# One decoder layer on one core: the output projection with its tokens stationary, the residual stream in rows, and the second norm's scale found beside its transposes

## The chip, the core and the metric

The kernel runs on one core of a Trainium2 chip. The metric is device microseconds of one execution. The kernel is written with a manual schedule: every engine works through its instructions in the order in which the Python code issues them. The engines are TensorE (PE in the profile, its weight loads PEld), VectorE (DVE), ScalarE (ACT), GpSimd (POOL) and SyncE (SP), which issues nearly all DMA transfers.

## The reference

One layer for 256 tokens (S) of width 2048 (D), all in fp32. `c` is one conditioning vector, and `mod` its six modulation vectors of width D.

```python
mod = (silu(c) @ ada_w + ada_b)                # sh1, sc1, g1, sh2, sc2, g2
h = rms_norm(x, norm1_g) * (1 + sc1) + sh1
u, lru_gate, q, k, v, mix_gates = split(h @ w_in + b_in)
y_lru  = rg_lru(causal_conv(u)) * gelu(lru_gate)
y_attn = sliding_window_attention(q, k, v, sinks)
gate_lru, gate_attn = split(sigmoid(mix_gates))
merged = gate_lru * (y_lru @ w_lru_out) + gate_attn * (y_attn @ w_attn_out)
x = x + g1 * (merged @ w_o)                    # called x1 below
h2 = rms_norm(x, norm2_g) * (1 + sc2) + sh2
gate, up = split(h2 @ w_ffn_in)
x = x + g2 * ((silu(gate) * up) @ w_ffn_out)
out = rms_norm(x, final_g)
```

The change concerns the line of `w_o` and the one that makes `h2`.

## The kernel before

**Products in three.** Each fp32 operand is split into a rounded "hi" and a remainder "lo", and a product is made as hi·hi + hi·lo + lo·hi (`mm3`, lines 319 to 321). The split of the activations is done once. The weights are split as they come.

**Items.** A weight matrix is cut into slabs of 512 output columns (`add_slab`), and a slab into items of 128 partitions x 1024 elements (512 KB), which hold two blocks of 128 contraction rows. Each item is loaded by SyncE into one of five buffers (`do_load`, tile `raw`, line 265), cast by ACT into `hi` (`do_hi`, line 274), subtracted by DVE into `lo` (`do_lo`, line 286), and multiplied. `step(i)` issues the load of item i+5, the cast and the subtraction of items a few ahead, and then the products of item i. So loads run five items ahead of the products. Eight items make a slab of 2048 contraction rows; a slab sums in two PSUM banks.

**Which operand stands.** `add_slab` has two forms. By default the weights are loaded into the array (128x128) and the 256 tokens move through: the result has output columns on the partitions and tokens along them. With `in_rows=True` the tokens are stationary, in two halves of 128, and 512 weight columns move: the result has tokens on the partitions. Tiles `wi`, `wl`, `wa` and `wo` are the banks of `w_in`, `w_lru`, `w_att` and `w_o`; `fg` and `fu` are the two halves of `w_ffn_in`. Up to the change w_o uses the first form, and w_att the second.

**Side work.** The modulation vectors are found meanwhile: 158 tiles `aw` of 512 KB are loaded from `ada_t` (line 377, three buffers) and each is multiplied with the spread `silu(c)` and summed in one DVE pass (line 406) into a column of `modc`, where `modc[:, m, kt]` is vector m (2 is g1, 3 is sh2, 4 is (1+sc2)·norm2_g) for output columns 128·kt onward. A planner keeps an estimated clock for each engine (`charge`, `load_time`) and puts such passes between items where its estimate has room; generators in `posts` (what is to be done after a slab: `o_post` for w_o) yield costs and are advanced once an item. What the planner decides is fixed when the program is built.

**Stages around the change.** The products of w_att (`wa`) begin at 656.6 us, those of w_o (`wo`) at 754.1 us, and those of w_ffn_in (`fg`) at 853.8 us. In w_o, `o_post(0)` issues four loads of x, transposed (`load_x`, line 123), behind the loads that `step` has issued by then; after each of the first three slabs DVE forms x1 = x + g1·(merged @ w_o) in place (line 958: g1 is a number for each partition), ACT squares it, and DVE adds the squares up over blocks into `fs`.

**The gap ahead of h2.** After the last slab `second_norm` has DVE finish x1, ACT square it, TensorE sum the squares over the partitions by products with a matrix of ones (tile `r`, lines 954 and 963; the sums come out spread over all partitions), ACT take the root (line 965), and DVE the reciprocal (line 966, 128x256). Then DVE scales (`scaled`, line 979) and ACT shifts and rounds (`high`, line 983) two blocks at a time, and DVE makes the remainders (`low`). h2 must have its first blocks before `fg` begins; the later blocks are made item by item in `rest`. Meanwhile TensorE transposes x1 back into rows (`rows_of`, line 934, 32 transposes), and ACT copies them out for writes to DRAM (`x1d`), from where the last stage reads x1.

Of the kernel before, what the change touches and what calls it, by code (L numbers as in the profile page):

```python
# [47 lines left out]

N_PIECES, N_F, K_FIRST = 3, 4, 3
# [16 lines left out]
def hybrid_layer(  # L66
    ctx: ExitStack, tc, vecs, x_t, c_row, ada_k, ada_t, ada_g, w_in, bv_row, bm_row, bg_row, lru_w, w_lru, w_att, w_o,
# [37 lines left out]
    def rows(t):  # L105
        return slice(t * P, (t + 1) * P)
# [32 lines left out]
    warm = mtile("warm")  # L139
    for _ in range(N_WARM):  # L140
        nc.tensor.matmul(warm[:, 0:P], lhsT=ones, rhs=ones, start=True, stop=True)
    free(m=1)
# [742 lines left out]
    for i in range(4):  # L885
        add_slab(w_in[SL_GA + i], f"wga{i}", hact, 0, NK, gate_post(SL_GA + i, i, ga), True, load_gate_bias(SL_GA + i), 4)
    for s in range(4):
        add_slab(w_att[s], f"wa{s}", aact, 0, NK, att_post(s), True)
# [3 lines left out]
    x1T, second = [], {}  # L892

    def o_post(s):
        def post(banks):
            if s == 0:
                x1T.extend(load_x("x1T"))
                second["fs"] = b4("fs2")
            if s == 3:
                second_norm(banks)  # L900
                return
            if s == 2:
                early_root()
            yield 0, 0
# [12 lines left out]
        return post  # L917
# [9 lines left out]
    pts = {}  # L927

    def rows_of(i, of_w=False):

        s, t = divmod(i, 2)
        pt = wtile(f"ptx{i}").rearrange("p j n -> p (j n)") if of_w else mtile(f"ptx{i}")
        for j in range(4):
            nc.tensor.transpose(pt[:, j * P:(j + 1) * P], x1T[s][:, j, rows(t)], ident)
        pts[i] = (pt, 0 if of_w else 1)

    def rows_out(i):
        s, t = divmod(i, 2)
        pt, m = pts.pop(i)
        xr = b4(f"xr{i}", F32, (512,))  # L940
        nc.scalar.copy(xr, pt)
        nc.sync.dma_start(x1d[rows(t), s * 512:(s + 1) * 512], xr)
        free(b4=1, m=m)
# [3 lines left out]
    def second_norm(banks):  # L947
        sides[:] = [ada_ffn]
        fs = second["fs"]
        both = h2["both"] = hp.tile([P, NK, 2, S], F32R, tag="h", name="h2_both")  # L950
        hh, hl = both[:, :, 0, :], both[:, :, 1, :]
        ps = mtile("r2_ps")[:, 0:S]
        for s in range(3):
            nc.tensor.matmul(ps, lhsT=ones, rhs=fs[:, s, :], start=s == 0, stop=False, skip_group_check=True)
        sq = b4("sq3")
        for f in range(4):
            xf = x1T[3][:, f, :]
            nc.vector.scalar_tensor_tensor(
                xf, banks[f // 2][:, f % 2, :], modc[:, 2, 12 + f:13 + f], xf, op0=ALU.mult, op1=ALU.add
            )  # L960
            nc.scalar.activation(sq[:, f, :], xf, AF.Square)
        for f in range(4):
            nc.tensor.matmul(ps, lhsT=ones, rhs=sq[:, f, :], start=False, stop=f == 3, skip_group_check=True)
        r2 = b4("r2")[:, 0, :]
        nc.scalar.activation(r2, ps, AF.Sqrt, bias=eps_t, scale=1.0 / D)
        nc.vector.reciprocal(r2, r2)
        free(m=1)

        for i in range(6):
            rows_of(i, i in (3, 4))  # L970
        for i in range(4):
            rows_out(i)
            if i < 2:
                rows_of(6 + i)

        def scaled(p):
            for kt in (2 * p, 2 * p + 1):
                xk = x1T[kt // 4][:, kt % 4, :]
                nc.vector.scalar_tensor_tensor(xk, xk, modc[:, 4, kt:kt + 1], r2, op0=ALU.mult, op1=ALU.mult)

        def high(p):
            for kt in (2 * p, 2 * p + 1):
                nc.scalar.activation(
                    hh[:, kt, :], x1T[kt // 4][:, kt % 4, :], AF.Identity, bias=modc[:, 3, kt:kt + 1]
                )

        def low(p):
            for kt in (2 * p, 2 * p + 1):
                nc.vector.scalar_tensor_tensor(
                    hl[:, kt, :], x1T[kt // 4][:, kt % 4, :], modc[:, 3, kt:kt + 1], f32(hh[:, kt, :]),  # L990
                    op0=ALU.add, op1=ALU.subtract,
                )

        def rest():
            for p in range(NK // 2):
                if 0 < p < 4:
                    rows_out(4 + p)
# [369 lines left out]
```

## Time and profile before

| | us |
|---|---|
| median of 3 runs | 1594.91 |
| lowest, highest | 1591.74, 1596.39 |
| the profiled execution | 1598.15 |
| its span | 1596.3 |
| its mean granted TensorE clock | 0.995 of full |

The profile is of one execution, and the times in its rows are microseconds from the start of its span. A row of a timeline gives the start, the time it took, the engine, the line, the operation with its output and inputs, a count if several like instructions stand in a row, and in brackets the idle time before it and what ended it. A product's row gives its whole passage through the array; the next one starts before it ends, so the spacing of starts is the time that a product costs. A line number is that of the program before. Bytes moved: 399.36 MB, 250 GB/s as a mean over the span.

### The profile page before, as it was taken

What the parts mean: (1) busy time and instruction counts of PE and PEld (TensorE: products, weight loads), DVE (VectorE), ACT (ScalarE), POOL (GpSimd) and SP (SyncE); (2) the same over time, 40 slices, a digit from 0 to 9 for tenths busy, and PEclk for the clock granted to TensorE, in tenths of its full rate; (3) what the DMA queues carried; (4) which work ended last, traced back from release to release, by engine and by line L of the source; (5) the groups of instructions that cost most, each with busy time, mean ns of one, the idle gap of its engine ahead of it and who ended that gap; (6) DMA issues with size and microseconds to landing.
All of it is one profiled execution on the core that took longest, in us unless ns stands there. A gap on an engine that the chain in (4) does not pass through costs nothing.

```text
span 1596.3 us, 22536 instructions
## 1 busy us (share of the span) xinstructions
PE 1571.4 (98%) x8522; PEld 1358.2 (85%) x8522; DVE 1124.5 (70%) x1427; ACT 770.2 (48%) x973; POOL 4.8 (0%) x9
## 2 busy tenths in 40 slices
PE   8999999999999999999999999999999999999997
PEld 5999999998888887878998887888888888888886
DVE  6789988989988888788757877445545544444465
ACT  4754444485965455333446444444444444333343
POOL 0000000000000000000000000000000000000000
PEclk9999999999999999999999999999999999999999
DMA  8998998767588778989967899666666666656553
GB/s 306 332 341 311 333 338 280 269 217 240 194 277 283 247 274 274 312 294 315 338 184 222 306 334 321 185 187 188 194 186 188 194 186 229 234 195 195 190 196 119
DMA packets 113586, 399.36 MB, mean 250 GB/s; under 512 B 12611, under 2 KB 13763, under 8 KB 113093
## 3 DMA queue, kind: packets, MB, share of 16 engines
q1 hardware_dynamic: 113190, 397.41, 75.2%
q8 instruction: 66, 1.08, 0.3%
q10 hardware_dynamic: 288, 0.52, 0.1%
q14 instruction: 42, 0.34, 0.1%
HBM read 393.69 MB, written 4.19 MB: 249 GB/s over the span
## 4 chain that ended last, share of the span: by engine, by line
PE 86%; DMA 8%; DVE 4%; issue 1%; ACT 0%; SPq 0%; DVEq 0%; ACTq 0%
PE pf L1089 11%; PE wi L321 6%; PE wi L319 6%; PE wi L320 6%; PE fg L319 4%; PE fg L320 4%; PE fg L321 4%; PE fu L320 4%; PE fu L321 4%; PE fu L319 4%; PE pl L1089 3%; DMA aw<-in_ada_t_dram 3%; DMA aw<-in_ada_g_dram 3%; PE wo L320 2%; PE wo L319 2%; PE wo L321 2%
## 5 line engine op out<-in xcount | busy, mean ns | idle before, releaser
L274 ACT CAST hi<-raw 128x1024 fp32r<-128x1024 f32 (+1 forms) x552 | 565.3, 1027 | 764.4 <-PE pf L1089 109.8
L286 DVE TENSOR_TENSOR lo<-raw,hi 128x1024 fp32r<-128x1024 f32 (+1 forms) x552 | 655.1, 1192 | 349.3 <-PE pf L1089 95.7
L321 PE MATMUL wi<-h_both,lo 128*128 128x256 f32 x784 | 222.1, 283 | 1.1 <-DVE lo L286 1.1
L319 PE MATMUL wi<-h_both,hi 128*128 128x256 f32 x784 | 222.6, 284 | 0.0
L320 PE MATMUL wi<-h_both,hi 128*128 128x256 f32 x784 | 221.8, 283 | 0.0
L321 PEld LDWEIGHTS wi<-h_both,lo 128*128 128x128 f32 x784 | 150.5, 192 | 1.5 <-DVE lo L286 1.5
L319 PEld LDWEIGHTS wi<-h_both,hi 128*128 128x128 f32 x784 | 150.5, 192 | 0.2
L320 PEld LDWEIGHTS wi<-h_both,hi 128*128 128x128 f32 x784 | 150.5, 192 | 0.2
L319 PE MATMUL fg<-hi,h_both 128*128 128x512 f32 x352 | 139.1, 395 | 0.0
L320 PE MATMUL fu<-lo,h_both 128*128 128x512 f32 x352 | 137.2, 390 | 1.0 <-DVE lo L286 1.0
L320 PE MATMUL fg<-lo,h_both 128*128 128x512 f32 x352 | 137.3, 390 | 0.0
L321 PE MATMUL fg<-hi,h_both 128*128 128x512 f32 x352 | 137.2, 390 | 0.0
L321 PE MATMUL fu<-hi,h_both 128*128 128x512 f32 x352 | 137.0, 389 | 0.0
L319 PE MATMUL fu<-hi,h_both 128*128 128x512 f32 x352 | 136.9, 389 | 0.0
L406 DVE CUSTOM_DVE_ANT_0 aw<-aw,crow,modc 128x1024 f32<-128x1024 f32 x79 | 101.1, 1281 | 19.3 <-DMA aw<-in_ada_t_dram 19.0
L406 DVE CUSTOM_DVE_ANT_0 aw<-aw,crow,vec 128x1024 f32<-128x1024 f32 x79 | 100.9, 1280 | 19.4 <-DMA aw<-in_ada_t_dram 19.1
L1089 PE MATMUL pf<-hi,fh 128*128 128x512 f32 x264 | 88.5, 389 | 0.0
L1089 PE MATMUL pf<-hi,fl 128*128 128x512 f32 x264 | 88.4, 389 | 0.0
L1089 PE MATMUL pf<-lo,fh 128*128 128x512 f32 x264 | 88.4, 389 | 0.0
L320 PEld LDWEIGHTS fu<-lo,h_both 128*128 128x128 f32 x352 | 66.1, 188 | 15.5 <-DVE lo L286 1.8
L320 PEld LDWEIGHTS fg<-lo,h_both 128*128 128x128 f32 x352 | 66.1, 188 | 14.6 <-issue 0.7
L319 PEld LDWEIGHTS fg<-hi,h_both 128*128 128x128 f32 x352 | 66.1, 188 | 14.2 <-issue 0.7
(233 smaller groups left out, 2615.1 us busy)
## 6 DMA issues: line engine op xcount, KB each, us to landing
raw<-in_w_f_dram SPq DMA_DIRECT2D x176, 512.0 KB, 3.6
raw<-in_w_in_dram SPq DMA_DIRECT2D x160, 512.0 KB, 6.8
aw<-in_ada_t_dram SPq DMA_DIRECT2D x158, 512.0 KB, 6.0
raw<-in_w_f2a_dram SPq DMA_DIRECT2D x44, 512.0 KB, 4.2
raw<-in_w_lru_dram SPq DMA_DIRECT2D x32, 512.0 KB, 6.6
raw<-in_w_att_dram SPq DMA_DIRECT2D x32, 512.0 KB, 7.7
raw<-in_w_o_dram SPq DMA_DIRECT2D x32, 512.0 KB, 6.5
aw<-in_ada_g_dram SPq DMA_DIRECT2D x32, 512.0 KB, 5.7
```

The source lines that it names most:

```text
L274: nc.scalar.copy(hi[:, :cols], live[i][0][:, :cols])
L286: nc.vector.tensor_tensor(lo[:, :cols], raw[:, :cols], f32(hi[:, :cols]), op=ALU.subtract)
L319: nc.tensor.matmul(ps, lhsT=lh, rhs=rh, start=start, stop=False, skip_group_check=True)
L320: nc.tensor.matmul(ps, lhsT=lh, rhs=rl, start=False, stop=False, skip_group_check=True)
L321: nc.tensor.matmul(ps, lhsT=ll, rhs=rh, start=False, stop=stop, skip_group_check=True)
L406: nc.vector.tensor_tensor_reduce(out=r, in0=r, in1=crow[:, j * CH:(j + 1) * CH], op0=ALU.mult, op1=ALU.add, scale=1.0, scalar=dst if j els ...
L1089: nc.tensor.matmul(fin[t, n], lhsT=l[:, rows(t)], rhs=w[:, c0:c0 + 512], start=kt == 0 and k == 0, stop=kt == (EARLY if (t, n) == (1, 3) e ...
```

## The change

1. w_o is computed in the second form: tokens stationary, 512 weight columns moving, so its banks hold rows (tokens on the partitions).
2. x is an input a second time, in rows (`x_r`, not transposed). Its four loads (`load_rows`, line 923, 512 KB each) are issued when the first item of w_o is multiplied, not after the first slab.
3. In rows, g1 is no longer one number for each partition, but a row that all partitions need. `gate_rows`, called as the second slab of w_att begins, transposes `modc[:, 2, :]` on TensorE, ACT copies it, an 8 KB DMA writes it to DRAM (`g1d`, line 904), and two DMAs read it back, spread over the partitions (line 907, 512 KB each).
4. `o_post` multiplies a bank by the gate row and adds x (two DVE lines), ACT squares each half with `accum_out`, so that the sum of squares of each token falls out as one number for each partition (`ss2`), and x1 is written to `x1d` straight from its rows (line 926) on SyncE.
5. The gap: x1 has to become columns for h2. `turn(p)` makes four transposes for two blocks; seven of the eight turns stand between w_o's last product and `fg`, the eighth in `rest`, after the first item of `fg`. Meanwhile the scale is found for each token as a number for each partition (`sr`: sum, root, reciprocal of 128x2), two diagonal matrices are made of it, and one product of ones with these (line 1004) spreads it along the partitions as `r2`. `keep_warm` issues 2 and 5 products without use around it (line 145).

The diff, cut to its core:

```diff
+    def keep_warm(n):
+        warm = wtile("warm")[:, 0, :]
+        for _ in range(n):
+            nc.tensor.matmul(warm[:, 0:P], lhsT=ones, rhs=ones, start=True, stop=True)
...
+    g1d = dp.tile([NK, P], F32, name="g1d")
+    def gate_rows():
+        while not {(2, kt) for kt in range(NK)} <= cols_done:
+            ada.advance(True)
+        ps = mtile("g1_ps")
+        nc.tensor.transpose(ps[0:NK, 0:P], modc[:, 2, :], ident)
+        row = sp.tile([P, S], F32, tag="t2", name="g1_row")
+        nc.scalar.copy(row[0:NK, 0:P], ps[0:NK, 0:P])
+        free(m=1)
+        nc.sync.dma_start(g1d, row[0:NK, 0:P])
+        for i in range(2):
+            g1.append(b4(f"g1{i}", F32, (CH,)))
+            nc.sync.dma_start(
+                g1[i], g1d[8 * i:8 * i + 8, :].rearrange("k p -> (k p)").partition_broadcast(P)
+            )
     for s in range(4):
-        add_slab(w_att[s], f"wa{s}", aact, 0, NK, att_post(s), True)
+        add_slab(w_att[s], f"wa{s}", aact, 0, NK, att_post(s), True, gate_rows if s == 1 else None)
...
+    def load_rows():
+        for s in range(4):
+            xr.append(b4(f"xr{s}", F32, (2, 512)))
+            nc.sync.dma_start(xr[s], x_r[:, s * 512:(s + 1) * 512].rearrange("(t p) n -> p t n", p=P))
+    def keep_rows(s):
+        nc.sync.dma_start(x1d[:, s * 512:(s + 1) * 512].rearrange("(t p) n -> p t n", p=P), xr[s])
     def o_post(s):
         def post(banks):
-            if s == 0:
-                x1T.extend(load_x("x1T"))
-                second["fs"] = b4("fs2")
...
-            for f in range(4):
-                xf = x1T[s][:, f, :]
-                nc.vector.scalar_tensor_tensor(
-                    xf, banks[f // 2][:, f % 2, :], modc[:, 2, 4 * s + f:4 * s + f + 1], xf,
-                    op0=ALU.mult, op1=ALU.add,
-                )
-            yield 1.3, 0
-            sq = b4(f"sq{s}")
-            nc.scalar.activation(sq, x1T[s], AF.Square)
-            yield 0, 0.95
-            nc.vector.tensor_reduce(second["fs"][:, s, :], sq.rearrange("p k s -> p s k"), axis=AX.X, op=ALU.add)
-            yield 1.14, 0
+            y = b4(f"yo{s}", F32, (2, 512))
+            for t in range(2):
+                nc.vector.tensor_tensor(y[:, t, :], in_rows_of(banks[t]), g1_of(s), op=ALU.mult)
+            yield 1.4, 0
+            nc.vector.tensor_tensor(xr[s], xr[s], y, op=ALU.add)
+            yield 1.13, 0
+            for t in range(2):
+                nc.scalar.activation(y[:, t, :], xr[s][:, t, :], AF.Square, accum_out=ss2[:, t, s:s + 1])
+            keep_rows(s)
+            free(b4=1)
+            yield 0, 1.6
...
-        add_slab(w_o[s], f"wo{s}", mact, 0, NK, o_post(s), before=x_first if s == 3 else None)
+        add_slab(w_o[s], f"wo{s}", mact, 0, NK, o_post(s), True, load_rows if s == 0 else x_first if s == 3 else None)
...
     def second_norm(banks):
...
+        for p in range(4):
+            turn(p)
+        y = b4("yo3", F32, (2, 512))
+        for t in range(2):
+            nc.vector.tensor_tensor(y[:, t, :], in_rows_of(banks[t]), g1_of(3), op=ALU.mult)
+            nc.vector.tensor_tensor(xr[3][:, t, :], xr[3][:, t, :], y[:, t, :], op=ALU.add)
+            nc.scalar.activation(y[:, t, :], xr[3][:, t, :], AF.Square, accum_out=ss2[:, t, 3:4])
+            if t == 0:
+                turned_copy(0, nc.scalar.copy)
+        keep_rows(3)
+        turn(4, True)
+        sr = sp.tile([P, 2], F32, tag="rc", name="sr")
+        turned_copy(1, nc.vector.tensor_copy)
+        nc.vector.tensor_reduce(sr, ss2, axis=AX.X, op=ALU.add)
+        nc.scalar.activation(sr, sr, AF.Sqrt, bias=eps_t, scale=1.0 / D)
+        nc.vector.reciprocal(sr, sr)
+        turn(5)
+        turn(6)
+        r2, diag = b4("r2")[:, 0, :], y[:, 0, 0:S]
+        nc.vector.tensor_scalar(diag[:, rows(0)], ident, sr[:, 0:1], None, op0=ALU.mult)
+        nc.scalar.activation(diag[:, rows(1)], ident, AF.Copy, scale=sr[:, 1:2])
+        r2_ps = wtile("r2_ps")[:, 0, :]
+        keep_warm(N_WARM_2[0])
+        nc.tensor.matmul(r2_ps, lhsT=ones, rhs=diag, start=True, stop=True)
+        keep_warm(N_WARM_2[1])
...
         def rest():
+            turn(7)
             for p in range(NK // 2):
...
-        scaled(0)
+        scaled(0, r2_ps)
         high(0)
-        rows_out(4)
+        nc.scalar.copy(r2, r2_ps)
```

What this does to the order is seen at three places. On SyncE, in w_att's second slab, before the change the loads of modulation (`aw`) and weights (`raw`) alternate:

```order
L265 DMA raw_6871<-in_w_att_dram 128x1024
L377 DMA aw_6877<-in_ada_t_dram 128x1024
L265 DMA raw_6893<-in_w_att_dram 128x1024
L377 DMA aw_6914<-in_ada_t_dram 128x1024
L265 DMA raw_6917<-in_w_att_dram 128x1024
L265 DMA raw_6935<-in_w_att_dram 128x1024
```

After it, the gate row's write and its two spread reads (`g1d`, `g`) stand between them:

```order
L270 DMA raw_6873<-in_w_att_dram 128x1024
L382 DMA aw_6879<-in_ada_t_dram 128x1024
L270 DMA raw_6895<-in_w_att_dram 128x1024
L904 DMA g1d<-g_row 16x128
L907 DMA g_6906<-g1d 128x1024
L907 DMA g_6908<-g1d 128x1024
L382 DMA aw_6925<-in_ada_t_dram 128x1024
L270 DMA raw_6928<-in_w_att_dram 128x1024
L270 DMA raw_6946<-in_w_att_dram 128x1024
```

The first `aw` and everything behind it on SyncE now come after the three new transfers. On SyncE in w_o, the loads of x before (`x1T`) stood behind w_o's thirteenth weight load, where no modulation load follows at once:

```order
L265 DMA raw_7657<-in_w_o_dram 128x1024
L265 DMA raw_7688<-in_w_o_dram 128x1024
L123 DMA x1T_7718<-in_x_t_dram 128x1024
L123 DMA x1T_7720<-in_x_t_dram 128x1024
L123 DMA x1T_7722<-in_x_t_dram 128x1024
L123 DMA x1T_7724<-in_x_t_dram 128x1024
L265 DMA raw_7727<-in_w_o_dram 128x1024
```

After the change the loads of x in rows (`xr`) stand behind the sixth:

```order
L382 DMA aw_7440<-in_ada_t_dram 128x1024
L270 DMA raw_7456<-in_w_o_dram 128x1024
L923 DMA xr_7462<-in_x_r_dram 128x2x512
L923 DMA xr_7464<-in_x_r_dram 128x2x512
L923 DMA xr_7466<-in_x_r_dram 128x2x512
L923 DMA xr_7468<-in_x_r_dram 128x2x512
L382 DMA aw_7485<-in_ada_t_dram 128x1024
L270 DMA raw_7488<-in_w_o_dram 128x1024
```

They moved by seven weight loads toward the start, and a modulation load is the next behind them. On TensorE in the gap, before the change the last product of w_o (`wo`) is followed by the sums of squares (`r_ps`), and these by the 32 transposes of x1 into rows (`ptx`), whose first is shown:

```order
L321 MATMUL wo_0_1_8234<-mh_7587,lo_8390 128x256
L954 MATMUL r_ps<-fs_7726,ones 128x256 x3
L963 MATMUL r_ps<-sq_8481,ones 128x256 x4
L934 MATMUL ptx_8497<-ident,x1T_7718 128x128 x4
L934 MATMUL ptx_8502<-ident,x1T_7718 128x128 x4
```

After it, seven turns (`pt`) come first, then the spare products (`warm`) and the one that spreads the scale (`r_ps`):

```order
L326 MATMUL wo_0_1_7959<-hi_8032,ml_7559 128x512
L965 MATMUL pt_8103<-ident,xr_7462 128x128 x4
L965 MATMUL pt_8108<-ident,xr_7462 128x128 x4
L965 MATMUL pt_8113<-ident,xr_7464 128x128 x4
L965 MATMUL pt_8118<-ident,xr_7464 128x128 x4
L965 MATMUL pt_8133<-ident,xr_7466 128x128 x4
L965 MATMUL pt_8144<-ident,xr_7466 128x128 x4
L965 MATMUL pt_8149<-ident,xr_7468 128x128 x4
L145 MATMUL warm<-ones 128x128 x2
L1004 MATMUL r_ps<-yo_8123,ones 128x256
L145 MATMUL warm<-ones 128x128 x5
L324 MATMUL fg_0_0_8192<-hi_8050,h_both 128x512
```

The transposes, which before need the finished x1 alone and come after the sums, now stand ahead of the product that gives the scale, and that one is the last thing of use before `fg`; the eighth turn stands twelve products later, after the first item of `fg`.

More of the change, by code (lines that the diff above doesn't have):

```diff
@@ L47 @@
 N_WARM = 4
+N_WARM_2 = (2, 5)
 N_PIECES, N_F, K_FIRST = 3, 4, 3
@@ L924, in hybrid_layer, with turn, turned_copy @@
     for s in range(4):
-        add_slab(w_o[s], f"wo{s}", mact, 0, NK, o_post(s), before=x_first if s == 3 else None)
[L927 to L943, printed above, removed]
+        add_slab(w_o[s], f"wo{s}", mact, 0, NK, o_post(s), True, load_rows if s == 0 else x_first if s == 3 else None)
+    def turn(p, of_w=False):
+        pt = wtile(f"pt{p}") if of_w else mtile(f"pt{p}").rearrange("p (j n) -> p j n", n=S)
+        for j in range(2):
+            for t in range(2):
+                c = (2 * p + j) % 4 * P
+                nc.tensor.transpose(pt[:, j, rows(t)], xr[p // 2][:, t, c:c + P], ident)
+        pts[p] = (pt, 0 if of_w else 1)
+    def turned_copy(p, eng):
+        pt, m = pts.pop(p)
+        x1T[p] = b4(f"x1T{p}", F32, (2, S))
+        eng(x1T[p], pt)
+        free(m=m)
     h2 = {}
@@ L962, in second_norm @@
[L962 to L979, printed above, removed]
+        for p in range(4):
+            turn(p)
@@ L981, in high @@
         def high(p):
[L982 to L985, printed above, removed]
+            for j in range(2):
+                kt = 2 * p + j
+                nc.scalar.activation(hh[:, kt, :], x1T[p][:, j, :], AF.Identity, bias=modc[:, 3, kt:kt + 1])
         def low(p):
-            for kt in (2 * p, 2 * p + 1):
+            for j in range(2):
+                kt = 2 * p + j
```

54 lines of the change are left out of this document (27 added, 27 removed).

## The prediction

> **What bounds the kernel now.** I read the page first (shares, chain), then the busy time by stretch, the waits between 650 and 860 us, and last the timelines of the three places that the change touches. Items are weight tiles of 128x1024, one load, one "hi" cast, one "lo" subtraction and one batch of products each; I count w_o's items from 1 to 32. In the page, the shares and the chain that ended last:
>
> ```profile
> PE 1571.4 (98%) x8522; PEld 1358.2 (85%) x8522; DVE 1124.5 (70%) x1427; ACT 770.2 (48%) x973; POOL 4.8 (0%) x9
> ...
> PE 86%; DMA 8%; DVE 4%; issue 1%; ACT 0%; SPq 0%; DVEq 0%; ACTq 0%
> ```
>
> TensorE's queue is nearly the whole time, so only what shortens TensorE's own work, or lets it stand still, counts. The stretches (stretch, length, busy us of PE, PEld, DVE, ACT, POOL, clock, DMA share, GB/s) are the stage wa, the time in which x's four loads are served inside w_o, and the rest of w_o:
>
> ```profile
> 656.60:754.00 97.40, 91.88 (x410) 74.10 (x409) 78.82 (x99) 36.50 (x38) 0.00 (x0) 1.00 0.91 304
> ...
> 783.00:792.00 9.00, 9.00 (x77) 9.00 (x77) 8.30 (x9) 4.21 (x4) 0.00 (x0) 1.00 1.02 408
> 792.00:847.00 55.00, 55.00 (x460) 55.00 (x460) 30.93 (x31) 24.01 (x25) 0.00 (x0) 1.00 0.62 183
> ```
>
> Two regimes show. In wa and during x's loads the DMA engines are 91 and 102% busy, and in wa TensorE lacks 5.5 of 97.4 us. From 792 us they are at 62%, and TensorE sets the pace. The waits between 650 and 860 us (total, times, longest) say what is late in the first regime:
>
> ```profile
> DVE aw L406 <- DMA aw<-in_ada_t_dram: 22.7, 17, 2.7
> ...
> PE wa L320 <- DVE lo L286: 5.4, 5, 1.6
> ```
>
> TensorE waits for DVE's "lo", and DVE, which works in order, waits for the modulation's weights ("aw") by DMA.
>
> **The change, part by part.** *Products.* The tile views of w_o and of a stage that already has its tokens stationary (name, count, min/median/max ns, first to last start):
>
> ```profile
> L320 PE MATMUL wo<-ml,hi x139: 283/283/283, 790.0 to 839.7; 128*128 128x256 f32 x139
> ```
> ```profile
> L320 PE MATMUL fg<-lo,h_both x21: 389/389/389, 861.7 to 875.3; 128*128 128x512 f32 x21
> ```
>
> w_o: 138 steps of three products in 49.7 us, 0.120 us a product, 2.88 us an item of 24. fg: 20 steps in 13.6 us, 0.2267 us a product of twice the width, 2.72 us an item of 12. So 32 items could save 32 x 0.16 = 5.1 us where TensorE sets the pace.
>
> *Gate row through DRAM.* The rows of before around the place of the new transfers. SyncE's load behind it and ACT's cast at it:
>
> ```profile
> 687.39 0.33 SPq L377 DMA_DIRECT2D aw<-in_ada_t_dram  x1
> ```
> ```profile
> 683.90 1.05 ACT L274 CAST hi<-raw 128x1024 fp32r<-128x1024 f32 x1 [0.24 <-DVE lo L286]
> ```
> DVE's modulation pass and its two "lo" behind, and the product that needs the first of them:
>
> ```profile
> 691.89 1.28 DVE L406 CUSTOM_DVE_ANT_0 aw<-aw,crow,vec 128x1024 f32<-128x1024 f32 x1
> ...
> 693.10 2.48 DVE L286 TENSOR_TENSOR lo<-raw,hi 128x1024 fp32r<-128x1024 f32 x2
> ```
> ```profile
> 695.81 0.39 PE L320 MATMUL wa<-lo,oh 128*128 128x512 f32 x1
> ```
>
> The nearest row for a write of this kernel to DRAM, x1's 256 KB writes after w_o:
>
> ```profile
> DMA to landing us min/median/max: 3.0/3.7/4.8
> ```
>
> The gate's transpose (about 0.1 us) and copy stand behind the cast of 683.90, so the copy ends near 685.3 and the 8 KB write is issued there. The writes take 3.0 to 4.8 us to land; I take 4.2, since loads are ahead of it in the queues, so 689.5. SyncE stands still meanwhile: the two broadcasts wait for the write, and behind them the aw of 687.39 and two raws. That aw goes out about 3.1 us late and behind 1 MB; at the 408 GB/s of the fullest stretch 512 KB take 1.285 us, so it lands near 695.6 instead of just before 691.89. DVE's "lo" of 693.10 sits behind it: 698.0 instead of 694.3, while its product was due at 695.81. TensorE loses 2.2 us. The Trainium skill, page "DMA: Bandwidth & Descriptors", section "Rules for kernel authors", says a DMA that reads what another wrote has to wait for the first one's completion, which is this stall; its fixed cost of about 2.0 us a DMA (section "Anatomy of one DMA — SWDGE (gpsimd) path") would make it, as an estimate, 2 us shorter. Later stalls of the same stage take a delay up:
>
> ```profile
> 708.24 0.50 PE L320 MATMUL wa<-lo,oh 128*128 128x512 f32 x1 [1.16 <-DVE lo L286]
> ...
> 712.41 0.50 PE L320 MATMUL wa<-lo,oh 128*128 128x512 f32 x1 [1.15 <-DVE lo L286]
> ...
> 728.84 0.50 PE L320 MATMUL wa<-lo,oh 128*128 128x512 f32 x1 [1.62 <-DVE lo L286]
> ```
>
> There TensorE waits 1.16, 1.15 and 1.62 us for "lo" anyway, 3.9 us in all, and after a hold-up the queue is shorter, so loads land sooner. What remains at 730 us is 0 (all taken up) to 3.7 us (the whole lateness of DVE's chain); I take 0.3.
>
> *x in rows.* The four loads of 512 KB move from behind w_o's thirteenth load to behind its sixth. Before, SyncE's queue:
>
> ```profile
> 756.05 0.38 SPq L265 DMA_DIRECT2D raw<-in_w_o_dram  x1
> 760.41 0.33 SPq L377 DMA_DIRECT2D aw<-in_ada_t_dram  x1
> ...
> 774.76 2.80 SPq L123 DMA_DIRECT2D x1T<-in_x_t_dram  x4
> 777.67 0.45 SPq L265 DMA_DIRECT2D raw<-in_w_o_dram  x1
> ```
> The cast of the load of 777.67, DVE's rows behind the aw of 760.41, and TensorE's first product of w_o and the eight transposes that stand in it:
>
> ```profile
> 788.07 1.05 ACT L274 CAST hi<-raw 128x1024 fp32r<-128x1024 f32 x1 [2.31 <-DMA raw<-in_w_o_dram]
> ```
> ```profile
> 766.57 1.28 DVE L406 CUSTOM_DVE_ANT_0 aw<-aw,crow,vec 128x1024 f32<-128x1024 f32 x1 [1.57 <-DMA aw<-in_ada_t_dram]
> ...
> 767.78 2.37 DVE L286 TENSOR_TENSOR lo<-raw,hi 128x1024 fp32r<-128x1024 f32 x2
> ```
> ```profile
> 754.12 0.28 PE L319 MATMUL wo<-mh,hi 128*128 128x256 f32 x1
> ...
> 762.75 0.49 PE L838 MATMUL mt<-ident,gate 128*128 128x128 f32 x3
> ```
>
> Right behind the four, a raw issued at 777.67 was cast at 788.07, 10.3 us later. Moved, the four go out from 756.8 to 759.6, and the aw of 760.41 stands where that raw stood: about 9.5 us to landing, 769.8, where DVE took it at 766.57 (1.57 us late already). DVE's two "lo" of 767.78 come 3.2 us later: the first, item 6's, ends at 772.2. With 2.72 us an item and 0.9 us of transposes (eight of 0.114, the rate of the row of 849.94 below) TensorE is at item 6 at 754.1 + 5 x 2.72 + 0.9 = 768.6, so it stands 3.4 us, and starts item 7 at 772.2 + 11/12 x 2.72 = 774.7, where before it was 754.1 + 6 x 2.88 + 0.9 = 772.3. That is +2.4. Behind it no x loads stand in the way (they cost the old order 777 to 788 us), and from there TensorE sets the pace: 26 items x 0.16 = -4.2. Bounds: with the loads hidden -4.3 to -5.1 in all, with nothing gained back +2.4. So w_o: -1.8.
>
> *The clock.* Stretches (columns as above) at the start, where TensorE had stood, and in wa:
>
> ```profile
> 28.59:32.00 3.41, 1.93 (x12) 1.33 (x11) 2.31 (x7) 2.36 (x5) 0.00 (x0) 1.00 0.89 237
> 32.00:35.42 3.42, 3.42 (x18) 3.42 (x18) 2.42 (x4) 0.20 (x1) 0.00 (x0) 0.50 1.02 399
> ...
> 677.12:680.54 3.42, 2.26 (x11) 1.54 (x9) 2.43 (x3) 1.05 (x1) 0.00 (x0) 1.00 0.90 314
> 680.54:683.95 3.41, 3.09 (x13) 2.21 (x13) 2.56 (x4) 1.10 (x2) 0.00 (x0) 1.00 0.94 291
> ```
>
> TensorE busy for 1.93 of 3.41 us was followed by 3.41 us at a clock of 0.50; busy for 2.26, by full clock. A stand of 3.4 us leaves one such stretch at most half busy, so the halved clock follows and takes 1.7 us. The one in wa (2.2 us) may do the same, and is taken up by the stalls shown. The Trainium skill, page "TensorE: Matmul & The Clock Gate", section "HAM oscillation — how this bites in real kernels", forbids only idle gaps of over about 3.4 us, by which neither would cost this (rival 2). I take the rows: +1.7.
>
> *The gap ahead of h2.* Before, from the last product (a row of several instructions gives the time of them all):
>
> ```profile
> 847.01 0.28 PE L321 MATMUL wo<-mh,lo 128*128 128x256 f32 x1
> ...
> 847.33 0.88 DVE L958 SCALAR_TENSOR_TENSOR x1T<-wo,modc,x1T 128x256 f32<-128x256 f32 x2 [0.56 <-PE wo L321]
> ...
> 849.94 3.63 PEld L934 LDWEIGHTS ptx<-ident,x1T 128*128 128x128 f32 x32
> ...
> 850.86 1.75 DVE L966 RECIPROCAL r<-r 128x256 f32<-128x256 f32 x1 [2.65 <-ACT r L965]
> ...
> 852.72 0.88 DVE L979 SCALAR_TENSOR_TENSOR x1T<-x1T,modc,r 128x256 f32<-128x256 f32 x2
> 853.24 0.91 ACT L983 ACTIVATE h_both<-x1T,modc 128x256 fp32r<-128x256 f32 x2 [0.40 <-DVE x1T L979]
> ...
> 853.80 0.50 PE L319 MATMUL fg<-hi,h_both 128*128 128x512 f32 x1
> ```
> The end of the kernel, which has the new chain (multiply, add, squares with sums, root, reciprocal) already:
>
> ```profile
> 1582.31 0.69 DVE L1101 TENSOR_TENSOR y<-pl,pa 128x512 f32<-128x512 f32 x1 [1.76 <-PE pl L1089]
> ...
> 1585.30 0.75 DVE L1149 SCALAR_TENSOR_TENSOR last<-last,r 128x512 f32<-128x512 f32 x1
> ```
>
> 6.79 us from the last product's start to fg's first. The long RECIPROCAL (1.75) and the rows' sums by products go; the new chain from multiply to first use of the root took 1582.31 to 1585.30, 2.99 us. With L the last product's start, the bank is ready at L + 0.45 (0.39 the product), the root at L + 3.44, the diagonal 0.4 later. TensorE is at L + 3.9 by then (28 transposes of 0.114, the row of 849.94, and two spare products of about 0.24), the column product takes 0.5, and scaled rows, "hi" and wake-up take the 1.08 us of 852.72 to 853.80: h2 at L + 5.5; five spare products end at L + 5.6. So -1.2. But the eighth turn now stands in TensorE's queue between fg's first and second item, and needs a bank that the third "scaled" frees. DVE's third is 3.72 us behind its first before (852.72, then 854.59 and 856.44 by the same spacing), so L + 4.5 + 3.7 + 0.9 = L + 9.1 against L + 8.55: a stand of 0.55 and 0.46 of transposes, +1.0. Net -0.2 (-1.2 to +0.8, if the diagonal comes late).
>
> *At nothing:* w_o's own additions on DVE (about 2.5 us a slab for 3.6) and the squares with their sums on ACT lie in a stretch where DVE has 31 of 55 us; the writes of x1 move there from the gap, beside a DMA at 62%. On SyncE each write waits for DVE's addition, about 3 us behind a slab's last product, with weight loads queued behind it; these run five items, 13.6 us, ahead of their products. Without that cover the squares would cost about 0.3 us a slab.
>
> *Sum:* +0.3 - 1.8 + 1.7 - 0.2 = 0.0. The profiled execution took 1598.15 us, span 1596.3; it is 3.2 above the median of 1594.91, which I move by the same amount: 1595 us.
>
> **The rivals.** *1, faster: the transfers are hidden.* x's early loads fill time in which DMA stood (97.4 us at 304 against 408 GB/s), DVE's chain is not late, and TensorE gets 4.4 of the 5.1 us (item 6's "lo" ended at 769.0 in before, 0.4 after the faster products want it, so the first items gain less) and 0.9 in the gap (of at most 1.2): -5.3, 1589.6. For it: the x loads before did run at 408. Against: the aw right behind them. Chance 0.24. *2, the clock stays full* beside the same stalls: -1.7, 1593.2, by the page's rule; the rows at 28.59 speak against it. 0.14. *3, slower: the two hold-ups add.* The gate row's 3.7 us stay in DVE's chain (no slack between 730 and 754), x's 2.4 come on top, and two stretches are halved: 3.7 + 2.4 - 4.2 + 3.4 - 0.2 = +5.1, 1600.0. It decides from where the aw's lateness at 728 us exceeds the 1.6 us of the last stall. Against: landings shorten after a hold-up. 0.20. *The forecast*, stalls as summed: 0.42.
>
> **How the numbers follow.** A measurement of this kernel cannot tell less than about 0.3%, 4.8 us, from no change. Rival 1 lies mostly beyond it (0.20 of 0.24), rival 3 too (0.18 of 0.20); the forecast and rival 2 lie within. Faster 0.21, same 0.60, slower 0.19. The range takes in most of rivals 1 and 3: 1589.3 to 1600.3; the forecast's own is 1592 to 1598.
>
> **What would show it.** Right: wo's products 0.2267 us apart; a TensorE stand near 696 us and one near w_o's sixth item, each followed by a clock below 1 in a 3.4 us stretch; w_o's first to last product as long as now within 2 us; the gap 5.5 to 5.8 us, then four transposes after fg's twelfth product. Wrong: w_o at 88 us with no stand (rival 1), or TensorE's loss in wa above 8 us and stands after 730 us (rival 3).

## The result, and the profile after

The changed kernel takes 1599.11 us (median of 20 runs, 1593.66 to 1604.55), the kernel before 1595.9 us (20 runs, 1590.16 to 1599.85). The ratio is 1.002, with a 95% interval of 1.0011 to 1.003: 3.2 us slower, between 1.8 and 4.8. The forecast was 1595.0, no change, in a range of 1589.3 to 1600.3. The time lies in the range, 4.1 us above the forecast's 1595.0 and outside the forecast's own 1592 to 1598. Of the 4.1 us, 3.2 are the change; the other 1.0 is the kernel before, whose median is 1595.9 in 20 runs and was 1594.91 in the first three runs. The prediction held that less than 4.8 us can't be told from no change; with 20 runs of each, 3.2 us can.

The profiled execution of the changed kernel took 1598.36 us with a span of 1596.6. The page, shares and chain:

```profile
PE 1568.1 (98%) x8141; PEld 1339.9 (84%) x8141; DVE 1121.8 (70%) x1424; ACT 767.8 (48%) x978; POOL 4.8 (0%) x9
...
PE 86%; DMA 8%; DVE 3%; issue 1%; ACT 1%; SPq 0%; DVEq 0%; ACTq 0%
```

TensorE is busy 3.3 us less than before, and the span is 0.3 us longer: what the products gained, TensorE stood. The stretches of 3.41 us around the two places where it stood (stretch, length, busy us of PE, PEld, DVE, ACT, POOL, clock, DMA share, GB/s):

```profile
695.10:698.51 3.41, 0.00 (x0) 0.00 (x0) 2.20 (x3) 0.37 (x1) 0.00 (x0) 1.00 1.01 369
698.51:701.93 3.42, 3.13 (x7) 2.48 (x8) 2.67 (x5) 2.59 (x4) 0.00 (x0) 0.50 1.03 419
770.19:773.61 3.42, 0.00 (x0) 0.00 (x0) 2.03 (x3) 0.78 (x1) 0.00 (x0) 1.00 1.02 408
773.61:777.02 3.41, 2.95 (x7) 2.38 (x8) 3.15 (x5) 2.56 (x5) 0.00 (x0) 0.50 0.91 308
```

In two stretches TensorE executes nothing, and in this execution the granted clock is 0.50 for one stretch behind each. Others lose more: the mean granted clock of the 20 runs is 0.9923, that of 74 runs of the kernel before, timed beside the experiments, 0.9950 (a further one, of 1946.55 us at a clock of 0.752, counts nowhere here). Over 1596 us that is 4.3 us of clock (an estimate from these means), or two and a half stretches of 1.7 us. What it waited for, on TensorE, ACT, DVE and SyncE at the first place:

```profile
693.69 0.39 PE L324 MATMUL wa<-hi,oh 128*128 128x512 f32 x1
698.80 0.80 PE L325 MATMUL wa<-lo,oh 128*128 128x512 f32 x1 [4.72 <-DVE lo L291]
```
```profile
684.16 0.24 ACT L902 COPY g_row<-g_ps 16x128 f32<-16x128 f32 x1
```
```profile
696.31 1.28 DVE L411 CUSTOM_DVE_ANT_0 aw<-aw,crow,vec 128x1024 f32<-128x1024 f32 x1 [5.77 <-DMA aw<-in_ada_t_dram]
...
697.52 1.22 DVE L291 TENSOR_TENSOR lo<-raw,hi 128x1024 fp32r<-128x1024 f32 x1
```
```profile
681.24 0.42 SPq L270 DMA_DIRECT2D raw<-in_w_att_dram  x1
684.42 0.33 SPq L904 DMA_DIRECT2D g1d<-g_row  x1
688.55 0.81 SPq L907 DMA_DIRECT2D g<-g1d  x2
689.46 0.38 SPq L382 DMA_DIRECT2D aw<-in_ada_t_dram  x1
```

Read from the last rows to the first: SyncE stands from 681.7 to 684.4 for the gate row's copy (on ACT behind two casts, it starts at 684.16). The reads of what the 8 KB write has written go out 4.1 us after it, and SyncE issues nothing between. It issues the next modulation load ("aw") at 689.46, behind 1 MB of spread reads. DVE waits 5.77 us for it, the "lo" behind it ends at 698.74, and TensorE starts again after 4.72 us. At the second place (TensorE, DVE, SyncE):

```profile
774.07 0.79 PE L325 MATMUL wo<-lo,mh 128*128 128x512 f32 x1 [3.94 <-DVE lo L291]
```
```profile
771.58 1.28 DVE L411 CUSTOM_DVE_ANT_0 aw<-aw,crow,vec 128x1024 f32<-128x1024 f32 x1 [6.20 <-DMA aw<-in_ada_t_dram]
...
772.79 2.35 DVE L291 TENSOR_TENSOR lo<-raw,hi 128x1024 fp32r<-128x1024 f32 x2
```
```profile
757.01 2.80 SPq L923 DMA_DIRECT2D xr<-in_x_r_dram  x4
760.79 0.34 SPq L382 DMA_DIRECT2D aw<-in_ada_t_dram  x1
```

An "aw" issued behind the four loads of x reaches DVE 10.8 us later, and TensorE stands 3.94 us for the "lo" behind it. The products themselves are as wide apart as forecast: in the tile view of w_o (count, min/median/max ns, first to last start), 73 steps of three products in 49.6 us, 0.2265 us a product.

```profile
L325 PE MATMUL wo<-lo,mh x74: 389/389/389, 789.9 to 839.5; 128*128 128x512 f32 x74
```

The gap ahead of h2, and the eighth turn (PE, DVE and ACT, in order of time):

```profile
848.56 0.39 PE L326 MATMUL wo<-hi,ml 128*128 128x512 f32 x1
...
851.98 0.40 ACT L1001 ACTIVATE yo<-ident,sr 128x128 f32<-128x128 f32 x1 [0.29 <-DVE sr L996]
...
852.44 0.70 PE L1004 MATMUL r_ps<-yo,ones 128*128 128x256 f32 x2
...
853.18 0.87 DVE L1013 SCALAR_TENSOR_TENSOR x1T<-x1T,modc,r_ps 128x256 f32<-128x256 f32 x2 [0.97 <-PE r_ps L1004]
853.75 0.91 ACT L1021 ACTIVATE h_both<-x1T,modc 128x256 fp32r<-128x256 f32 x2 [1.37 <-DVE x1T L1013]
...
854.32 0.50 PE L324 MATMUL fg<-hi,h_both 128*128 128x512 f32 x1
...
857.02 0.40 PE L326 MATMUL fg<-hi,h_both 128*128 128x512 f32 x1
...
857.88 0.66 PE L965 MATMUL pt<-ident,xr 128*128 128x128 f32 x4 [0.46 <-DVE x1T L1013]
...
858.29 0.48 PE L324 MATMUL fg<-hi,h_both 128*128 128x512 f32 x1
```

From the last product's start to fg's first the gap takes 5.76 us, where before it took 6.79. The eighth turn waits 0.46 us for a bank, and fg's thirteenth product starts 1.27 us after its twelfth instead of 0.23.

### The profile page after: what moved, and what is told of

Read it like the earlier page. It is cut to its first block, busy times and chain, and to the rows that moved or that the text cites. A ratio compares the mean times of both kernels' runs of the same rounds, so it can differ in the third digit from the quotient of the medians.

```text
span 1596.6 us, 21759 instructions
## 1 busy us (share of the span) xinstructions
PE 1568.1 (98%) x8141; PEld 1339.9 (84%) x8141; DVE 1121.8 (70%) x1424; ACT 767.8 (48%) x978; POOL 4.8 (0%) x9
## 3 DMA queue, kind: packets, MB, share of 16 engines
q8 instruction: 63, 1.03, 0.3%
## 4 chain that ended last, share of the span: by engine, by line
PE 86%; DMA 8%; DVE 3%; issue 1%; ACT 1%; SPq 0%; DVEq 0%; ACTq 0%
PE pf L1127 11%; PE wi L326 6%; PE wi L325 6%; PE wi L324 6%; PE fg L325 4%; PE fg L324 4%; PE fg L326 4%; PE fu L325 4%; PE fu L326 4%; PE fu L324 4%; PE pl L1127 3%; DMA aw<-in_ada_g_dram 3%; DMA aw<-in_ada_t_dram 2%; PE wga L326 2%; PE wl L325 2%; PE wl L326 2%
## 5 line engine op out<-in xcount | busy, mean ns | idle before, releaser
L411 DVE CUSTOM_DVE_ANT_0 aw<-aw,crow,modc 128x1024 f32<-128x1024 f32 x79 | 100.9, 1279 | 16.2 <-DMA aw<-in_ada_t_dram 16.1
```

What stands on the lines that cost most here:

```text
L411: nc.vector.tensor_tensor_reduce(out=r, in0=r, in1=crow[:, j * CH:(j + 1) * CH], op0=ALU.mult, op1=ALU.add, scale=1.0, scalar=dst if j els ...
```

## The experiments

The theory after the result: the change as such is worth about 5 us, and two transfers queued on SyncE ahead of modulation loads cost more than that. Rivals: w_o's faster products can't be fed in any case; the stands are taken up later; the halved clock, not the stand, is what costs. Lengths of stages below are from first product to first product (w_att, "wa"), first to last product (w_o), and last product to fg's first (gap), from one profile each. Ratios are to the kernel before, timed on the same chip, with 95% intervals: 20 runs of the changed kernel, 5 of "spread out", 12 of each other kernel that has a ratio. A difference between two rows carries the uncertainty of both, 2.2 to 2.7 us either way (an estimate from the intervals). Lengths vary from one execution to the next; the profiles of "gate read later" and "spares in w_o's stand" are the fastest of their 12 runs.

| kernel | ratio | us to before | wa | w_o | gap |
|---|---|---|---|---|---|
| before | | | 97.3 | 92.9 | 6.79 |
| before, second profile | | | 94.9 | 93.5 | 6.78 |
| changed | 1.0020 (1.0011 to 1.0030) | +3.2 | 98.1 | 93.3 | 5.76 |
| changed, second profile | | | 97.4 | 94.8 | 5.75 |
| x by slab | 0.9992 (0.9981 to 1.0004) | -1.3 | 97.2 | 89.7 | 5.75 |
| gate read later | 1.0006 (0.9995 to 1.0018) | +1.0 | 94.4 | 94.3 | 5.75 |
| both later | 0.9963 (0.9951 to 0.9975) | -5.9 | 93.6 | 91.2 | 5.75 |
| spread out | 0.9963 (0.9949 to 0.9977) | -5.9 | 95.9 | 90.5 | 5.75 |
| gate alone (on before) | 1.0008 (0.9995 to 1.0021) | +1.3 | 98.0 | 92.9 | 6.78 |
| x early alone (on before) | 1.0018 (1.0006 to 1.0030) | +2.9 | 94.6 | 99.8 | 6.79 |
| spares in both stands | 1.0022 (1.0012 to 1.0032) | +3.5 | 100.9 | 92.8 | 5.75 |
| spares in w_o's stand | 1.0008 (0.9997 to 1.0019) | +1.3 | 96.6 | 92.8 | 5.75 |
| no spares in the gap | | | 96.9 | 94.8 | 5.75 |

**x slab by slab.** Each load of x goes behind the sixth weight load that follows the start of its own slab.

```diff
-    def load_rows():
-        for s in range(4):
-            xr.append(...); nc.sync.dma_start(xr[s], ...)
+    def load_rows(s):
+        xr.append(...); nc.sync.dma_start(xr[s], ...)
...
-        add_slab(w_o[s], ..., True, load_rows if s == 0 else x_first if s == 3 else None)
+        add_slab(w_o[s], ..., True, x_first(s))          # load_rows(s), and for s == 3 ada.finish too
```

> The changed kernel with x's four loads in rows issued one by one, each behind the sixth weight load that follows the start of its own slab of w_o, in place of all four in the first slab. Theory (the stand at w_o's sixth item is a modulation load queued behind the four x loads): the stand of 4.1 us falls below 1 us, the clock stays full in w_o, and w_o takes 88 to 89 us from first to last product in place of 93.3; time about 5 us below the changed kernel, near 1594. Rival (the faster products are short of weights by themselves while modulation loads run): a stand of over 3 us stays in w_o's first ten items, and the time moves by less than 1.5 us.

Measured: 4.5 us below the changed kernel by the ratios (1595.02 us median), clear of the 2.4 us of uncertainty. TensorE's longest wait in w_o fell from 3.94 to 1.37 us, and it is one for the "lo" part of w_att's result (`ml`), not for weights:

```profile
774.19 0.50 PE L326 MATMUL wo<-hi,ml 128*128 128x512 f32 x1 [1.37 <-DVE ml L852]
```

The clock stayed full in w_o, which took 89.7 us. The theory holds, though w_o is about 1 us longer than it said and a wait of 1.37 us is left where it said under 1; the rival that the products can't be fed falls.

**The gate's reads later.** Transpose, copy and write stay in w_att's second slab; the two reads go to the start of the third.

```diff
         nc.sync.dma_start(g1d, row[0:NK, 0:P])
+    def gate_spread():
         for i in range(2):
             g1.append(b4(f"g1{i}", F32, (CH,)))
...
-        add_slab(w_att[s], ..., gate_rows if s == 1 else None)
+        add_slab(w_att[s], ..., {1: gate_rows, 2: gate_spread}.get(s))
```

> The changed kernel with the two spread reads of the gate row issued at the start of w_att's third slab; the transpose, the copy and the 8 KB write stay in the second, so SyncE no longer waits for the write's landing. Theory (the later stalls of w_att take the hold-up up anyway): the stand of 4.9 us near 694 us and the halved clock behind it go, but stalls of 1 to 2 us return behind it as in the kernel before, and w_att takes 97 to 98 us in place of 98.1; time within 1.5 us of the changed kernel. Rival (the hold-up is on the path): w_att 92 to 94 us, time 4 to 6 us lower.

Measured: 2.2 us below the changed kernel by the ratios, with 2.4 us of uncertainty either way, so between the theory's 1.5 and the rival's 4 to 6 it decides nothing. The stand of 4.7 us is gone, and TensorE stands 1.7 and 1.5 us behind it instead. w_att took 94.4 us, against the theory's 97 to 98, in the fastest of the 12 runs.

**Both.** The two edits together.

> The edits of the kernel with x's loads slab by slab and of the one with the gate's reads later, together. Theory: the sum of both, about 5 to 6 us below the changed kernel (near 1593.5), with w_o at 88 to 89 us from first to last product and w_att at 97 to 98 us. Rival (both stands lie on the path): 9 to 11 us below the changed kernel. Rival (w_o is short of weights by itself): within 2 us of the changed kernel.

Measured: 1590.73 us, 8.4 below the changed kernel's median and, by the ratios, 9.1 below it (2.4 either way) and 5.9 us below before. The theory's sum of 5 to 6 us is a miss; what came is the rival, that both stands lie on the path. Against the kernel with x by slab alone, the gate's later reads are worth 4.6 us here (2.7 either way), clear of noise, where beside the early loads of x they gave 2.2. Whether the two hold-ups hide a part of each other isn't shown: the 2.4 us between these figures are within their uncertainty. w_att (93.6 us) and w_o (91.2) missed the expected 97 to 98 and 88 to 89. No stretch of halved clock lies between 50 and 1580 us. DVE's waits for "aw" between 650 and 860 us, of the changed kernel and of this one (total, times, longest):

```profile
DVE aw L411 <- DMA aw<-in_ada_t_dram: 27.5, 17, 6.2
```
```profile
DVE aw L411 <- DMA aw<-in_ada_t_dram: 20.6, 21, 2.3
```

**Further apart.** The write goes to w_att's third slab, the two reads to its fourth slab and to w_o's second; the eighth turn goes behind fg's second item.

```diff
-        {1: gate_rows, 2: gate_spread}
+        {1: gate_rows, 2: gate_write, 3: lambda: gate_spread(0)}      # gate_spread(1) in w_o's second slab
...
         def rest():
-            turn(7)
             for p in range(NK // 2):
+                if p == 1:
+                    turn(7)
```

> The kernel with both transfers later, and further: the gate row's write at the start of w_att's third slab, when its copy is long done, its two halves read at the start of w_att's fourth slab and of w_o's second slab; the eighth turn after the second item of fg in place of the first. Theory (what is left of the cost is SyncE's wait for the copy, 2.8 us, the second 512 KB among the modulation loads, and the stand of 0.6 us before the eighth turn): 1 to 2 us below the kernel with both later, 1589 to 1590. Rival (nothing of that is on the path): 1590.7, within 0.5 us.

Measured: 1591.0 us, the same ratio as with both later: the theory is a miss, the rival came. The eighth turn no longer waits for its bank, but DVE still waits 23.2 us for "aw" between 650 and 860 us (22.7 in the kernel before), and TensorE in small stands for the "lo" behind. That the modulation loads bind w_att and w_o's first slab, whatever the gate's transfers do, fits this; no run tests it. Nor does a run separate SyncE's wait for the write from the reads' 1 MB: to move the reads ends the wait and moves the 1 MB at once.

**The gate's transfers alone.** `gate_rows` as in the changed kernel, added to the kernel before, its result not used.

> The kernel before with the gate row's transfers added as the changed kernel has them (transpose, copy, 8 KB write, two spread reads at the start of w_att's second slab), their result not used; w_o, x's loads and the gap are those of before. Theory (the gate's hold-up of SyncE and its 1 MB lie mostly on the path, as the 2.8 us that moving the reads gave say): 2.5 to 4.5 us slower than before (ratio 1.0016 to 1.0028), with a stand of 4 to 5 us near 694 us. Rival (the stand is taken up by w_att's later stalls, as the prediction had it): within 1 us of before.

Measured: +1.3 us (interval -0.8 to +3.4), between theory and rival; the interval holds values of both. The stand is there:

```profile
697.73 0.79 PE L320 MATMUL wa<-lo,oh 128*128 128x512 f32 x1 [3.87 <-DVE lo L286]
```

**x early alone.** `load_x("x1T")` of the kernel before moved to the start of w_o's first slab, the queue position of the changed kernel.

> The kernel before with its four loads of x moved from behind w_o's thirteenth weight load to behind its sixth, where the changed kernel has its own; everything else, the weights-stationary products among it, is that of before. Theory (what costs is a modulation load queued behind 2 MB of x, whatever form the products have): a stand of 3 to 5 us at w_o's sixth or seventh item with a halved clock behind it, w_o 95 to 97.5 us from first to last product in place of 93, time 2 to 4 us above before. Rival (the early place is free by itself and only the faster products make it a stand): no stand above 1.5 us, within 1 us of before.

Measured: +2.9 us (+1.0 to +4.8). With the old products too, DVE waits 5 us for an "aw" behind the four loads, TensorE stands for "lo", and in the profiled execution the clock is halved, for two stretches:

```profile
769.48 1.28 DVE L406 CUSTOM_DVE_ANT_0 aw<-aw,crow,vec 128x1024 f32<-128x1024 f32 x1 [5.03 <-DMA aw<-in_ada_t_dram]
```
```profile
771.97 0.58 PE L321 MATMUL wo<-mh,lo 128*128 128x256 f32 x1 [2.97 <-DVE lo L286]
```
```profile
771.04:774.46 3.42, 2.49 (x11) 2.49 (x12) 3.29 (x5) 2.69 (x5) 0.00 (x0) 0.50 0.95 322
774.46:777.87 3.41, 3.41 (x18) 3.41 (x17) 3.13 (x6) 0.97 (x1) 0.00 (x0) 0.50 0.91 291
```

w_o took 99.8 us, more than expected; the profiled execution was the longest of this kernel's 12 (1602.13 us against a median of 1598.97). The two halved stretches explain it: 27 products behind the stand take 5.92 us, where at 0.120 us each they would take 3.24, so the clock cost 2.7 us. With the stand of 3.1 and another stall of 1.0 this makes 6.8 us; w_o is 6.7 us longer than the 93.1 of the old queue. On average the 12 runs lost less to the clock: its mean is 0.9945, that of before beside them 0.9949, which is 0.6 us of 1596.

**Both kernels again.**

> The kernel before, unchanged, for a second profile. Theory (w_att's 97.3 us of the first profile are typical of before): 96.5 to 98 us. Rival (that execution was a slow one in w_att, which hides the cost of the gate's transfers in a comparison of two profiles): 93 to 95.5 us.

> The changed kernel, unchanged, for a second profile: a stand of 4 to 5 us at the same two items (w_att's fourteenth and w_o's sixth), a halved clock behind each, w_att 98 us and w_o's first product to fg's first 99 us, each within 1 us. If the stands are elsewhere or differ by over 2 us, they are chance and not the queue's order.

The kernel before took 94.9 us in w_att this time: the 97.3 of the first profile were the longer of its two, and hid the gate's cost in a comparison of two profiles. The changed kernel stood at the same two items again (4.8 and 4.0 us from start to start; 5.1 and 4.3 in the first profile), with a halved clock behind each, but now for two stretches each. In w_o:

```profile
770.02:773.43 3.41, 2.24 (x5) 1.83 (x6) 3.15 (x3) 2.90 (x4) 0.00 (x0) 0.50 0.96 345
773.43:776.85 3.42, 3.42 (x9) 2.65 (x8) 3.42 (x6) 1.39 (x2) 0.00 (x0) 0.50 0.96 328
```

So w_o's first product to fg's first took 100.6 us, 0.6 beyond the expected 98 to 100.

**Spare products in the stands.** The first of mm3's products is followed by products without use, at the item named only.

```diff
         nc.tensor.matmul(ps, lhsT=lh, rhs=rh, start=start, stop=False, skip_group_check=True)
+        if between:
+            spare = mtile("spare")
+            for _ in range(between):
+                nc.tensor.matmul(spare[:, 0:P], lhsT=ones, rhs=ones, start=True, stop=True)
+            free(m=1)
```

> The changed kernel with products without use put between the first and the second product of the two items at which TensorE stood: 14 at w_att's fourteenth item (3.3 us of 4.9), 11 at w_o's sixth (2.6 us of 4.1). Nothing else moves. Theory (a stand that leaves a 3.4 us stretch mostly idle is followed by a halved clock, and only w_o's costs time, since later stalls of w_att take up the other): no stretch of halved clock between 50 and 1580 us, w_att's length unchanged within 0.5 us, w_o 1.7 us shorter; time 1.7 us below the changed kernel. Rival 1 (both halved stretches cost): 3.4 us lower. Rival 2 (weights are late behind the stand anyway, so the clock costs nothing): no difference.

> The changed kernel with the 11 products without use at w_o's sixth item alone. The changed kernel's w_o took 93.3 and 94.8 us from first to last product. Theory (a halved clock behind w_o's stand costs 1.7 us): full clock in w_o, 92.0 to 93.0 us, time 1.7 us below the changed kernel. Rival (at full clock TensorE only reaches the next late weights sooner): full clock in w_o, new stalls of 1 to 2 us between 778 and 795 us, w_o 93.3 to 94.8 us as before, time within 0.7 us of the changed kernel.

Measured, with spares at both places: no halved clock between 50 and 1580 us, w_o 92.8 us; but the time was 0.3 us above the changed kernel's, where the theory had 1.7 below, and w_att took 100.9 us in a profile that was 3.2 us above its kernel's median. With spares in w_o alone: 1.9 us below the changed kernel by the ratios (2.3 either way), w_o 92.8 us again, as the theory had it. The spares (each of the 11 products stands as two instructions) and the stand that was left:

```profile
767.94 2.62 PE L328 MATMUL spare<-ones 128*128 128x128 f32 x22
772.03 0.50 PE L330 MATMUL wo<-lo,mh 128*128 128x512 f32 x1 [1.48 <-DVE lo L291]
```
```profile
772.80:776.20 3.40, 3.39 (x15) 2.44 (x15) 3.14 (x6) 2.01 (x3) 0.00 (x0) 1.00 0.91 276
```

The stand is no shorter in all (2.6 us of spares and 1.5 of waiting), but the clock behind it is full, and w_o is 1.5 us shorter than in the mean of the four profiles that have the stand without spares (93.3, 94.8, 94.3, 94.8; mean 94.3). The spacing of the products says the same: behind w_o's stand, the halved clock cost 1.5, 2.8, 1.8 and 1.7 us in these four (2.8 where two stretches were halved). In w_att its price is not settled: spares there kept the clock full and gained nothing, and the kernel with both was 2.2 us slower than with spares in w_o alone (2.4 either way).

**No spare products in the gap.** `N_WARM_2 = (0, 0)`.

> The changed kernel without the 2 and 5 spare products in the gap ahead of h2. Theory (TensorE stands for 0.5 and 1.3 us without them, too little of a 3.4 us stretch to halve the clock): the gap is 5.7 us as with them, and the clock stays full behind it. Rival (they keep the clock up): a stretch of halved clock begins between 853 and 859 us.

One execution was taken. The gap is 5.75 us without them, and no halved clock follows it. With 0.43 and 1.17 us of standing left in the gap, they change nothing here:

```profile
850.78 0.70 PE L1004 MATMUL r_ps<-yo,ones 128*128 128x256 f32 x2 [0.43 <-ACT yo L1001]
852.66 0.50 PE L324 MATMUL fg<-hi,h_both 128*128 128x512 f32 x1 [1.17 <-ACT h_both L1021]
```

## Why the prediction was nearly right, step by step

| step | forecast | measured | from |
|---|---|---|---|
| gate row in w_att | +0.3 (0 to +3.7) | +1.3, +2.2 or +4.6 | gate alone; gate read later against the changed kernel; both later against x by slab |
| w_o, with the clock | -1.8 + 1.7 = -0.1 | +1.2 | w_o's length: mean 94.3 of four profiles with the early loads, 93.1 of three of the old form |
| gap's chain | -1.2 | -1.03 | last product to fg's first |
| eighth turn | +1.0 | +1.04 | fg's twelfth to thirteenth product |
| sum | 0.0 | +2.5 to +5.8 | timed: +3.2 (1.8 to 4.8) |

*The mechanism was right.* Both stands are at the items that were named, w_att's fourteenth and w_o's sixth, behind the loads named, each followed by a halved clock; the prediction counted one stretch each, and the second profile has two. The gap's two terms came out within 0.2 us. That the time kept within the range owes nothing to errors that cancel: the gate's term and w_o's were both too small, and the range was wide enough, 11 us, for both.

*The gate's term was too small.* The write took 4.1 us until its reads went out (taken: 4.2) and the "aw" reached DVE at 696.31 (taken: 695.6). But the stand was 4.7 us, not 2.2: the due time of 695.81 came from one execution in which TensorE had lost 1.8 us at 680 and 684 us, and was late itself; the changed kernel did not lose them and wanted the "lo" from 693.9 (0.23 behind the row of 693.69). Later stalls took up part, as the step said: behind the stand the changed kernel waited 0.50 us once, where before it waited 1.16, 1.15 and 1.62. But they did not take up nearly all. The same execution made w_att look 97.3 us long, where two other profiles with the old queue have 94.9 and 94.6, so the stalls counted as room for the hold-up were larger than usual. How large the term is stays open between 1.3 and 4.6 us.

*In w_o the stand was longer, and more came on top.* The "aw" needed 10.8 us to reach DVE, where 9.5 were taken although the row beside it showed 10.3. The gain of the products came in full: 384 of them 0.2265 us apart, for 768 at 0.120, are 5.1 us less. Against it stood, in the mean of the four profiles with the early loads, a stand of 4.1 us (from start to start, less a product's 0.23; forecast 3.4), 1.9 us of halved clock (forecast 1.7), and another wait in two of the four (0.3 and 1.0 us). So w_o with its early loads was not 0.1 us shorter but 1.2 longer.

*The rivals.* Rival 1 describes the change once the transfers don't stand ahead of modulation loads, and its total fits: -5.9 us for both later, -5.3 in the rival. Its terms don't, so that is in part luck: w_o is 1.9 to 3.4 us shorter (91.2, 90.5 and 89.7 in three kernels with x by slab, against 93.1), not 4.4, and with both later the eighth turn takes back the 1.0 us that the gap gains. Where the rest of the 5.9 us comes from is open. Rival 2 falls: the clock was halved behind both stands in both profiles of the changed kernel, and the stand with spares inside had none. Rival 3 had the right direction, with the hold-ups adding up; its +5.1 lies just above the measured interval. Its 3.7 us for the gate lie among the measured 1.3 to 4.6; for a halved clock in w_att that counts in full no run here speaks. As for the rule of the Trainium skill, page "TensorE: Matmul & The Clock Gate", section "HAM oscillation — how this bites in real kernels" (gaps of over about 3.4 us of idle): the two stands of the changed kernel, 4.7 and 3.9 us, fall under it and agree; x early alone has a stand of 2.97 us with a halved clock behind it, and there the measurement goes further than the rule.

## What to carry to other kernels

In a queue like SyncE's here, a new transfer delays what stands behind it: look for the consumer of the next load in the queue, not of the new one, and put transfers that have time (here x) one by one between the loads. SyncE issued no load while the reads behind it waited for a write (4.1 us here); write early, and read so much later that the write has landed. A term that depends on stalls in one profile (a due time, room that takes up a delay) needs a second profile: here w_att's length moved by 2.5 us between two executions of the kernel before, and the changed kernel's halved stretches from one to two.

## What the runs showed of the hardware that was not expected

Putting 2.6 us of products without use into a stand of 4.1 us kept the clock full and made w_o 1.5 us shorter, at no cost in the stand itself; what that gave in the whole time (1.9 us) isn't clear of its 2.3 us of uncertainty. And the gap ahead of h2 needs no such products: with stands of 0.43 and 1.17 us in it the clock stayed full.

How long a stretch TensorE was busy did not alone decide the clock behind it, as the prediction's two rows (1.93 and 2.26 of 3.41 us) suggest. With the gate read later, a stretch busy for 1.54 us was followed by full clock, and in the changed kernel one busy for 2.20 us by 0.50:

```profile
762.76:766.17 3.41, 1.54 (x7) 0.94 (x5) 0.00 (x1) 0.00 (x0) 0.00 (x0) 1.00 1.03 409
766.17:769.58 3.41, 0.93 (x4) 0.78 (x5) 3.41 (x4) 2.17 (x4) 0.00 (x0) 1.00 1.01 382
```
```profile
29.50:32.91 3.41, 2.20 (x14) 1.60 (x13) 1.98 (x5) 2.56 (x5) 0.00 (x0) 1.00 0.83 232
32.91:36.33 3.42, 3.42 (x18) 3.42 (x18) 2.53 (x5) 0.00 (x0) 0.00 (x0) 0.50 1.00 389
```

What decides between them is open.
